# HGRN level scores by blocks of 64 keys, and retention decode states in the third weight set

## The chip, the cores and the metric

The kernel runs on one core of one Trainium2 chip. The metric is the device time of one execution in microseconds. The program before was run three times; the median is 1087.16 us. One more execution was taken by the hardware profiler. TensorE (PE) does the matmuls and its weight loads (PEld), VectorE (DVE) and ScalarE (ACT) the elementwise work, GpSimd (POOL) a little of it, and SyncE (SP) issues most DMAs.

## The reference

One inference step of a decoder layer, all in fp32: 2048 prompt tokens from an empty state, and 8 decode sequences of one token each, which start from stored states. The width is 1024. Four heads of 128 are RetNet retention (a fixed decay per head), four are HGRN2 (a forget gate per channel and token).

```python
h = rmsnorm(x, norm_g)
p = (h @ w_in).astype(jnp.float32)
rq, rk, rv, rg, hq, hf, hi, hgate = jnp.split(p, 8, axis=-1)
...
o_ret, s_ret_new = chunked_decay_recurrence(rq, rk, rv, log_gamma, s_ret)
o_ret = head_rmsnorm(o_ret, ret_g) * jax.nn.silu(rg)
...
logf = jnp.logaddexp(jnp.log(lbf), jnp.log1p(-lbf) + jax.nn.log_sigmoid(hf))
kin = (1.0 - lbf) * jax.nn.sigmoid(-hf)
hq_act = jax.nn.silu(hq)
o_hg, s_hg_new = chunked_decay_recurrence(
    hq_act.reshape(B, L, HG_HEADS, HG_DK), kin.reshape(B, L, HG_HEADS, HG_DK),
    hi.reshape(B, L, HG_HEADS, HG_DV), logf.reshape(B, L, HG_HEADS, HG_DK), s_hg)
o_hg = head_rmsnorm(o_hg, hg_g) * jax.nn.silu(hgate)
...
o_cat = jnp.concatenate([o_ret, o_hg], axis=-1).astype(x.dtype)
y = x + o_cat @ w_out
```

The recurrence of a head is S_t = diag(f_t) S_{t-1} + k_t v_t^T with o_t = S_t^T q_t. Results are the normed outputs of the prompt and of the decode tokens, and the new states of both.

## The kernel before

**Stages.** Matmuls of the large products are done in F32R with each operand split into a high and a low part, three products in place of one. The first 578 us project the prompt, pair by pair of 128-token chunks, with seven block products per pair (the list CHAIN, run by v_pair); eight pairs make one weight set. The first set (token pairs i = 0 to 7) gives values and decode projections, the second (8 to 15) the retention queries and gates, the third (16 to 23) the retention keys and the HGRN gates. In the third set the retention of the prompt runs along, one step between two block products (r_steps: r_flip transposes the keys into pkt, r_score and r_update make par and pur, r_out makes por and rS and the normed output obr, r_turn transposes it into potr). What is not done by its end is the list tail_f, which is emptied between the first projection steps of the scan (the list early).

Then comes the scan: eight units, one per HGRN head and half of the prompt. A unit projects its gate and query (pjf, pjq, line 879), while the unit before it is worked through by hgrn_rec. The output projection (py, po) ends the program.

**Levels.** Within a chunk of 128 tokens, hgrn_rec builds the matrix A of scores by levels: level b (1, 2, 4, ..., 64) holds the pairs whose query is in an odd block of b tokens and whose key is in the even block before it. After each level, update scales keys and queries by the products of the gates, in place. The five small levels, 1 to 16, are made by small: before, a chunk is cut into four blocks of 32 keys, and each is a matmul of 32 keys (the stationary operand, 128 rows by 32 columns) with the 16 queries of odd blocks among the same 32 tokens. Each fp32 matmul is two instructions with two weight loads. The four blocks of a chunk write to four ranges of 32 partitions in one bank of PSUM. What the level's mask allows is copied by put into the tile Ab (copy_predicated, line 1091). scores0 does the diagonal (pd, through the unit matrix id32) and level 1; scores(1) levels 2 and 4; scores(3) levels 8 and 16; scores3 levels 32 and 64 (p5 and p6) and the copies into A on ACT. They stand at fractions 0.08, 0.3, 0.52 and 0.74 of a unit, in bursts: all 64 or 128 small matmuls in a row. keep sets a copy of keys and queries aside for the first of two levels.

**Decode heads.** A head's decode state is a tile dS of 128 by 8 by 128. d_load fetches it and the values vb (dv), d_mul and d_add compute the new state on DVE, and d_mm stores it and multiplies it by the query (pd, line 563), copies the result (de) and writes it to d_dram. Before, all eight heads stand in the list side_at at places in units 4 to 7.

**What sets the order.** TensorE's order is the order of the program text. On the other engines a scheduler places instructions by their dependencies; behind(f) ties what f emits to what was last emitted on DVE, ACT and SP. Tiles of a pool with one tag share buffers in turn.

Of the kernel before, what the change touches and what calls it, by code (L numbers as in the profile page):

```python
# [18 lines left out]
P = 128  # L19
# [13 lines left out]
PACK = dict(gk=4, gkd=4, epsg=4, ng=8, hg_lb=8, id32=32, xs_t=64, lmask=16 * len(SMALL), causal=P)  # L33
# [8 lines left out]
def step_kernel(ctx, tc, a, out):  # L42
# [55 lines left out]
    gk, gkd, ng, epsg, causal, id32 = (packed(n) for n in ("gk", "gkd", "ng", "epsg", "causal", "id32"))  # L98
# [5 lines left out]
    lmask = const.tile([P, len(SMALL) * 16], U8, name="lmask")  # L104
# [570 lines left out]
    dve.tensor_copy(lmask, packed("lmask"))  # L675
# [106 lines left out]

    n_tok = len(TOK)
    SPLIT_AT = 3
    for i in range(2, n_tok):
# [232 lines left out]
    def hgrn_rec(half, h, u):  # L1018
# [53 lines left out]
        def small(dst, li, ss=None):  # L1072
            b = LEVELS[li]
            m = 32 // (2 * b)
            for c in range(CH):
                for i in range(4):
                    at = c * P + 32 * i
                    if ss is None:
                        kk = k[:, at : at + 32]
                        n0 = (c * 4 + i) * m  # L1080
# [4 lines left out]
                    pe.matmul(dst[32 * i : 32 * i + 32, c], kk, qq, start=True, stop=True)  # L1085

        def put(src, li):
            b = LEVELS[li]
            m = 32 // (2 * b)
            mk = lmask[:, li * 16 : (li + 1) * 16].rearrange("p (n b) -> p n b", b=b)  # L1090
            dve.copy_predicated(
                box["Ab"].rearrange("p c (n two b) -> p c n two b", two=2, b=b)[:, :, :, 1, :],
                mk.unsqueeze(1).to_broadcast([P, CH, m, b]),
                src.rearrange("p c (n b) -> p c n b", b=b),
            )

        def scores0():
            box["Ab"] = pools["up"].tile([P, CH, 32], F32, tag="Ab", name=f"Ab{name}")
            pa = ps_lv.tile([P, 2, CH, 32], F32, tag="lv", name=f"pa{name}")
            pd, p0 = pa[:, 0], pa[:, 1, :, :16]  # L1100
            for c in range(CH):
                for i in range(4):
                    cc = slice(c * P + 32 * i, c * P + 32 * i + 32)
                    pe.matmul(pd[32 * i : 32 * i + 32, c], k[:, cc], q[:, cc], start=True, stop=True)
            small(p0, 0)
            update(0)
            products()
            dve.tensor_tensor(
                box["Ab"], pd, id32.unsqueeze(1).to_broadcast([P, CH, 32]), op=ALU.mult
            )  # L1110
            put(p0, 0)
            keep(1)

        def scores(li):
            pl = ps_lv.tile([P, 2, CH, 16], F32, tag="lv", name=f"pl{name}{li}")
# [7 lines left out]
        def scores3():  # L1123
# [81 lines left out]
    dec = {}  # L1205

    def d_load(hd):
        ty, h = divmod(hd, NH)
        S = rawp.tile([P, NB, P], F32, tag="raw", name=f"dS{hd}")
        vb = rawp.tile([P, NB, P], F32, tag="raw", name=f"dv{hd}")  # L1210
        sp.dma_start(S, (a["state_ret"], a["state_hgrn"])[ty][0, :, h].rearrange("b d v -> d b v"))
        sp.dma_start(vb, vd_dram[ty, :, h * P : (h + 1) * P].partition_broadcast(P))
        dec["l", hd] = (S, vb)

    def d_mul(hd, n):
        ty, h = divmod(hd, NH)
        S, vb = dec["l", hd]
        if n == 0:
            kd = dk[:, hd].unsqueeze(2).to_broadcast([P, NB, P])
            dve.tensor_tensor(vb, vb, kd, op=ALU.mult)  # L1220
        elif ty == 1:
            fd = df[:, hd].unsqueeze(2).to_broadcast([P, NB, P])
            dve.tensor_tensor(S, S, fd, op=ALU.mult)

    def d_add(hd):
        ty, h = divmod(hd, NH)
        S, vb = dec["l", hd]
        if ty == 0:
            dve.scalar_tensor_tensor(S, S, GAMMA[h], vb, op0=ALU.mult, op1=ALU.add)
        else:  # L1230
            dve.tensor_tensor(S, S, vb, op=ALU.add)
        if hd == 0:
            dec["q"] = pools["up"].tile([P, 8, 32], F32, tag="dqp", name="dqp")
            dve.tensor_copy(dec["q"][:, :, 8:32], zero.unsqueeze(1).to_broadcast([P, 8, 24]))
            dve.tensor_copy(dec["q"][:, :, 0:8], dq)

    def d_mm(hd):
        S, vb = dec["l", hd]
        ty, h = divmod(hd, NH)
        sp.dma_start(out[("new_ret_sample", "new_hgrn_sample")[ty]][0, :, h].rearrange("b d v -> d b v"), S)  # L1240
        e = pools["tp"].tile([P, 512], F32, tag="tmp", name=f"de{hd}")
        pt = ps_o.tile([P, 256], F32, tag="o", name=f"pd{hd}")
        four(pt, dec["q"][:, hd], S.rearrange("p b d -> p (b d)"), True, True)
        act.activation(e[:, :256], pt, AF.Copy)
        for i in range(2):
            act.dma_start(d_dram[hd, i::2], e[i : i + 103 : 34, i * P : i * P + P])

# [54 lines left out]
    for hd, at in enumerate((4.22, 5.01, 5.24, 6.01, 6.16, 6.31, 7.01, 7.22)):  # L1302
# [107 lines left out]
    for i in range(len(order)):  # L1410
# [4 lines left out]
        if i == 0:  # L1415
# [306 lines left out]
def _layout(x_prompt, x_sample, state_ret, state_hgrn, norm_g, w_in, ret_norm_g, hg_norm_g,  # L1722
# [41 lines left out]
    arrays["id32"] = (i[:, None] % 32 == i[None, :32]).astype(f32)  # L1764
    masks = []
    s32 = i % 32
    for b in SMALL:
        t = np.array([x for x in range(32) if (x // b) % 2 == 1])
        masks.append((s32[:, None] // b + 1) == (t[None, :] // b))
# [24 lines left out]
```

## Time and profile before

| | us |
| --- | --- |
| three runs | 1086.08, 1087.16, 1093.3 |
| median | 1087.16 |
| profiled execution | 1087.88 |
| its span | 1086.1 |
| TensorE busy (page, part 1) | 1043.2 |
| DVE busy | 760.8 |
| ACT busy | 553.3 |

The profile is of one execution. Its span is the time from the first to the last instruction; 1.8 us of the execution lie outside it. "Busy" of TensorE counts time in which at least one matmul is in flight by the profiler's model. In the rows of groups, "128*32" is the shape of the weights, what follows it the operand; "x1024" counts instructions; after the bar stand the group's busy time, the mean nanoseconds of one instruction, the idle time just before them and what ended it. Buffer numbers are left out of names, so pl of unit h00 is plh.

### The profile page before, as it was taken

How to read it: one execution, taken by the hardware profiler on the slowest of the kernel's cores; microseconds unless marked ns; L12 is line 12 of the kernel's file. 1: busy time of each engine (PE TensorE's matmuls, PEld its weight loads, DVE VectorE, ACT ScalarE, POOL GpSimd, SP SyncE). 2: the span in 40 equal slices, each digit the busy share in tenths (PEclk: the TensorE clock that was granted, in tenths of full speed). 3: DMA queues.
4: the chain of work that ended last, by engine and by line, in shares of the span. 5: the costliest groups of instructions: out<-in, count | busy, mean ns of one | idle time of the engine just before them, and what ended most of it. 6: DMA issues, size and time to landing. Idle time of an engine off the chain costs nothing.

```text
span 1086.1 us, 22296 instructions
## 1 busy us (share of the span) xinstructions
PE 1043.2 (96%) x8743; PEld 860.5 (79%) x8743; DVE 760.8 (70%) x1400; ACT 553.3 (51%) x1204; POOL 127.9 (12%) x224
## 2 busy tenths in 40 slices
PE   9999999999999999999999989899999998999997
PEld 7778778787778788888887968787887877888775
DVE  6876765987667876666656676768657786568776
ACT  7853444643344755455555655565545573523242
POOL 1310001000001011111111100011012011221112
PEclk9999999999999999999999999999999998999999
DMA  8689989668769865555567686767577483496652
GB/s 296 209 296 318 339 286 324 229 221 302 257 225 285 290 228 175 162 172 174 168 204 273 211 287 221 282 192 228 182 211 214 141 269 110 130 357 200 213 172 97
DMA packets 147130, 248.34 MB, mean 229 GB/s; under 512 B 10608, under 2 KB 78464, under 8 KB 146768
## 3 DMA queue, kind: packets, MB, share of 16 engines
q1 hardware_dynamic: 139424, 221.34, 61.5%
q0 software_dynamic: 7328, 25.27, 6.6%
q8 instruction: 69, 1.13, 0.4%
q14 instruction: 37, 0.30, 0.1%
q10 hardware_dynamic: 272, 0.30, 0.1%
HBM read 162.32 MB, written 84.54 MB: 227 GB/s over the span
## 4 chain that ended last, share of the span: by engine, by line
PE 65%; DMA 13%; DVE 8%; ACT 7%; issue 4%; POOL 2%; SPq 1%; DVEq 0%; POOLq 0%; ACTq 0%
PE po L332 11%; PE pjfh L879 5%; PE pjqh L879 5%; DMA xn<-in_x_prompt 4%; PE py L1502 4%; DMA qt_dram<-qt 2%; PE par L702 1%; PE plh L1085 1%; PE pur L709 1%; PE por L715 1%; PE puh L960 1%; DMA wr<-in_w_in 1%; PE poh L976 1%; PE por L717 1%; DMA wg1B<-in_w 1%
## 5 line engine op out<-in xcount | busy, mean ns | idle before, releaser
L879 PE MATMUL pjqh<-xh,w_h 128*128 128x512 f32 (+2 forms) x160 | 60.5, 378 | 2.9 <-DVE qh L930 1.9
L879 PE MATMUL pjfh<-xh,w_h 128*128 128x512 f32 (+2 forms) x160 | 59.9, 374 | 0.0
L879 PE MATMUL pjfh<-xh,w_l 128*128 128x512 f32 (+2 forms) x160 | 57.0, 356 | 0.7 <-DVE w_l L116 0.7
L879 PE MATMUL pjfh<-xl,w_h 128*128 128x512 f32 (+2 forms) x160 | 57.2, 357 | 0.4 <-DVE xl L116 0.3
L1065 ACT ACTIVATE kepth<-kh 128x1024 f32<-128x1024 f32 x24 | 25.4, 1060 | 62.0 <-DVE kh L1055 58.2
L879 PE MATMUL pjqh<-xl,w_h 128*128 128x512 f32 (+2 forms) x160 | 56.7, 354 | 0.0
L879 PE MATMUL pjqh<-xh,w_l 128*128 128x512 f32 (+2 forms) x160 | 56.6, 354 | 0.0
L1055 DVE TENSOR_TENSOR kh<-kh,fph 128x512 f32<-128x512 f32 x48 | 33.4, 696 | 21.3 <-PE plh L1085 11.3
L116 DVE TENSOR_TENSOR ab_l<-xr,ab_h 128x512 fp32r<-128x512 f32 (+1 forms) x40 | 37.5, 953 | 6.9 <-ACT ab_h L115 6.9
L731 DVE SCALAR_TENSOR_TENSOR obr<-por,omr,rg 128x128 f32<-128x128 f32 x64 | 18.0, 344 | 34.1 <-POOL omr L729 34.1
L115 ACT ACTIVATE ab_h<-xr 128x512 fp32r<-128x512 f32 (+1 forms) x40 | 32.3, 840 | 17.1 <-DVE xr L286 17.0
L987 DVE SCALAR_TENSOR_TENSOR obh<-poh,orsh,v 128x128 f32<-128x128 f32 x64 | 18.0, 344 | 30.9 <-POOL orsh L112 30.9
L879 PEld LDWEIGHTS pjqh<-xh,w_h 128*128 128x128 f32 x160 | 30.6, 191 | 8.5 <-DVE qh L930 2.1
L879 PEld LDWEIGHTS pjfh<-xh,w_l 128*128 128x128 f32 x160 | 30.8, 192 | 5.9 <-DVE w_l L116 1.6
L879 PEld LDWEIGHTS pjfh<-xh,w_h 128*128 128x128 f32 x160 | 30.6, 191 | 5.5 <-issue 1.2
L879 PEld LDWEIGHTS pjfh<-xl,w_h 128*128 128x128 f32 x160 | 30.8, 193 | 4.3 <-DVE xl L116 1.0
L879 PEld LDWEIGHTS pjqh<-xh,w_l 128*128 128x128 f32 x160 | 30.7, 192 | 4.3
L286 DVE SCALAR_TENSOR_TENSOR xr<-xr,g_in,rb 128x256 f32<-128x256 f32 x64 | 26.7, 479 | 10.4 <-DMA xr<-in_x_t 5.0
L879 PEld LDWEIGHTS pjqh<-xl,w_h 128*128 128x128 f32 x160 | 30.8, 192 | 3.0
L1058 DVE TENSOR_TENSOR qth<-qth,fph 128x512 f32<-128x512 f32 x48 | 32.8, 684 | 0.0
L742 ACT ACTIVATE obr<-potr,pk 128x128 f32<-128x128 f32 x64 | 19.0, 368 | 21.7 <-PE potr L740 21.7
L1592 DVE SCALAR_TENSOR_TENSOR xro<-xro,yms,fg 128x1024 f32<-128x1024 f32 (+1 forms) x13 | 15.5, 1202 | 18.5 <-POOL yms L112 18.5
(1836 smaller groups left out, 3426.4 us busy)
## 6 DMA issues: line engine op xcount, KB each, us to landing
xr<-a_dram SPq DMA_DIRECT2D x24, 512.0 KB
S<-s_dram SPq DMA_DIRECT2D x24, 512.0 KB
xn<-in_x_prompt SPq DMA_DIRECT2D x32, 256.0 KB
xr<-in_x_t SPq DMA_DIRECT2D x16, 512.0 KB
a_dram<-xr SPq DMA_DIRECT2D x16, 512.0 KB
s_dram<-S SPq DMA_DIRECT2D x16, 512.0 KB
wgr<-in_w SPq DMA_DIRECT2D x16, 512.0 KB
xr<-a_dram SPq DMA_DIRECT2D x32, 256.0 KB
```

The costliest lines, as they stand in the source:

```text
L115: act.activation(h, src, AF.Copy)
L116: dve.tensor_tensor(l, src, h.bitcast(F32), op=ALU.subtract)
L286: dve.scalar_tensor_tensor(r[:, k], r[:, k], g_in[:, kk : kk + 1], spread_to[i], op0=ALU.mult, op1=ALU.mult)
L332: pe.matmul(ps, xx, ww, start=(first and n == 0), stop=(last and n == 2), skip_group_check=more)
L731: dve.scalar_tensor_tensor(o[:, cc], po[:, h], ms[:, h : h + 1], rb_of[c, "g"][:, cc], op0=ALU.mult, op1=ALU.mult)
L742: act.activation(o[:, cc], pt[:, h], AF.Copy, scale=ng[:, h : h + 1])
L879: pe.matmul(ps, ww[:, kk], x[:, k, b0 : b0 + n], start=(k == 0 and i == 0), stop=(k == KT - 1 and i == 2),)
L987: dve.scalar_tensor_tensor(ob[g][:, j], po[:, j], rs[:, j : j + 1], gcol(4 * g + j), op0=ALU.mult, op1=ALU.mult)
L1055: dve.tensor_tensor(kv[:, :, 0, :], kv[:, :, 0, :], two[:, :, 1:2].to_broadcast([P, nb, b]), op=ALU.mult)
L1058: dve.tensor_tensor(qv[:, :, 1, :], qv[:, :, 1, :], two[:, :, 0:1].to_broadcast([P, nb, b]), op=ALU.mult)
L1065: act.activation(ss[:, 512:], k[:, :HALF], AF.Copy)
L1502: pe.matmul(ps, o[:, kk], w[:, k % 4, i * 512 : (i + 1) * 512], start=(k == 0 and n == 0), stop=(k == KT - 1 and n == 2),)
```

## The change

**Blocks of 64 keys.** small cuts a chunk into two blocks of 64 keys, each multiplied by the 32 queries of odd blocks among the same 64 tokens. There are 640 such matmuls in place of 1280, in two column groups in place of four. Ab is 64 wide; put writes 256 elements per partition in place of 128; the diagonal, which stays in blocks of 32, is multiplied into Ab in two halves by id64; two copies bring Ab into A, and they stand before the copies of p5 and p6.

On TensorE, at the first burst of the first scan unit, the row pah (line 1104) is the diagonal and the next row level 1. Before:

```order
L879 MATMUL pjfh_512_5761<-xl_5561,w_h 128x256
L879 MATMUL pjfh_512_5761<-xh_5560,w_l 128x256
L1104 MATMUL pah_5775<-qh_5590,kh_5589 32x32 x32
L1085 MATMUL pah_5775<-qth_5591,kh_5589 32x16 x32
L879 MATMUL pjfh_512_5761<-xh_5560,w_h 128x256
L879 MATMUL pjfh_512_5761<-xl_5561,w_h 128x256
```

And with the change, where the lines are 63 further on:

```order
L942 MATMUL pjfh_512_5830<-xl_5630,w_h 128x256
L942 MATMUL pjfh_512_5830<-xh_5629,w_l 128x256
L1167 MATMUL pah_5844<-qh_5659,kh_5658 32x32 x32
L1148 MATMUL pah_5844<-qth_5660,kh_5658 64x32 x16
L942 MATMUL pjfh_512_5830<-xh_5629,w_h 128x256
L942 MATMUL pjfh_512_5830<-xl_5630,w_h 128x256
```

The burst stands at the same place; its second half is 16 matmuls with an output of 64 by 32 in place of 32 with one of 32 by 16. The bursts of scores(1) and scores(3) change alike.

**Retention decode heads.** The functions d_load to d_mm move up in the text, ahead of the loop over token pairs, and the four retention heads run with token pairs 18 to 22 of the third set: a load after block product 3, the multiplication after 4, the addition after 6, and the matmul after product 1 of the next pair, in a bank of the pool ps_tr. The HGRN heads stand at 4.4, 5.1, 5.9 and 6.6 of the scan. d_dram is written from SP's queue in place of ACT's. The load of a token pair's operands comes after product 5 in the third set, as in the second, in place of 2.

On TensorE, where pair 19 passes from its second to its third product, potr and pkt are transposes of the retention, pv19 products of the pair, and pd the decode matmul of head 0. Before:

```order
L740 MATMUL potr_4041<-ident,obr_3986 128x128 x4
L332 MATMUL pv19b<-wv_h,ab_h 128x512
L332 MATMUL pv19b<-wv_l,ab_h 128x512
L332 MATMUL pv19b<-wv_h,ab_l 128x512
L332 MATMUL pv19b<-wv_h,ab_h 128x512
L332 MATMUL pv19b<-wv_l,ab_h 128x512
L332 MATMUL pv19b<-wv_h,ab_l 128x512
L694 MATMUL pkt_4065<-ident,rk_4008 128x128 x4
L332 MATMUL pv19a<-T2h,s190h 128x512
```

And with the change:

```order
L742 MATMUL potr_4052<-ident,obr_3996 128x128 x4
L332 MATMUL pv19b<-wv_h,ab_h 128x512
L332 MATMUL pv19b<-wv_l,ab_h 128x512
L332 MATMUL pv19b<-wv_h,ab_l 128x512
L332 MATMUL pv19b<-wv_h,ab_h 128x512
L332 MATMUL pv19b<-wv_l,ab_h 128x512
L332 MATMUL pv19b<-wv_h,ab_l 128x512
L696 MATMUL pkt_4076<-ident,rk_4018 128x128 x4
L563 MATMUL pd_4088<-dS_3897,dqr 32x256 x4
L332 MATMUL pv19a<-T2h,s190h 128x512
```

pd stands between pkt and the next product, as it does in the three pairs that follow.

On DVE, from the retention of pair 18 to the keys of pair 19 (rS and obr belong to the retention, rk and t to the keys), before:

```order
L721 SCALAR_TENSOR_TENSOR rS<-rS,pur_3941 128x128 x4
L731 SCALAR_TENSOR_TENSOR obr_3986<-por_3973,omr_3987,rg_3920 128x128 x4
L349 TENSOR_TENSOR t_4009<-pv18a,rot_3744 128x512
L352 TENSOR_TENSOR t_4010<-pv18a,rot_3744 128x4x64
L353 SCALAR_TENSOR_TENSOR t_4010<-pv18a,rot_3744 128x4x64
L354 TENSOR_TENSOR rk_4008<-t_4009,t_4010 128x512
L384 TENSOR_TENSOR rk_4057<-pv19b,s_19_4030 128x512
```

And with the change, where dv and dS are head 0's values and state:

```order
L723 SCALAR_TENSOR_TENSOR rS<-rS,pur_3951 128x128 x2
L800 TENSOR_TENSOR dv_3898<-dv_3898,dk 128x1024
L723 SCALAR_TENSOR_TENSOR rS<-rS,pur_3951 128x128 x2
L733 SCALAR_TENSOR_TENSOR obr_3996<-por_3983,omr_3997,rg_3929 128x128 x4
L349 TENSOR_TENSOR t_4019<-pv18a,rot_3746 128x512
L352 TENSOR_TENSOR t_4020<-pv18a,rot_3746 128x4x64
L353 SCALAR_TENSOR_TENSOR t_4020<-pv18a,rot_3746 128x4x64
L354 TENSOR_TENSOR rk_4018<-t_4019,t_4020 128x512
L809 SCALAR_TENSOR_TENSOR dS_3897<-dS_3897,dv_3898 128x1024
L384 TENSOR_TENSOR rk_4068<-pv19b,s_19_4041 128x512
```

The multiplication of dv parts the four rS and stands ahead of obr; the addition into dS stands between the two keys.

**Smaller edits.** The mask lmask comes from an input of its own through a tile in vq, no longer out of the packed constants pk. A spare tile, fill, grows from 104 to 120 floats. As built, the tiles of the pools xp, wp, rawp, vq, vp, tp and up start at multiples of 512 bytes; before, 64 bytes beyond one. Of the list early, the entries after which a step of tail_f runs are 0, 1, 4, 6, 8 and 11 in place of 0, 1, 3, 5, 7 and 11.

```diff
-    gk, gkd, ng, epsg, causal, id32 = (packed(n) for n in ("gk", "gkd", "ng", "epsg", "causal", "id32"))
+    gk, gkd, ng, epsg, causal, id64 = (packed(n) for n in ("gk", "gkd", "ng", "epsg", "causal", "id64"))
...
-    const.tile([P, 104], F32, name="fill")
+    const.tile([P, 120], F32, name="fill")
...
-    dve.tensor_copy(lmask, packed("lmask"))
+    lm = vq.tile([P, GW], F32, tag="rv", name="lm")[:, : len(SMALL) * 32]
+    sp.dma_start(lm, a["lmask"])
+    dve.tensor_copy(lmask, lm)
...
+    def d_mm(hd):
+        S, vb = dec["l", hd]
+        ty, h = divmod(hd, NH)
+        sp.dma_start(out[("new_ret_sample", "new_hgrn_sample")[ty]][0, :, h].rearrange("b d v -> d b v"), S)
+        if ty:
+            e = pools["tp"].tile([P, 512], F32, tag="tmp", name=f"de{hd}")
+            pt = ps_o.tile([P, 256], F32, tag="o", name=f"pd{hd}")
+        else:
+            e = vq.tile([P, GW], F32, tag="xn", name=f"de{hd}", bufs=2)
+            pt = ps_tr.tile([P, 256], F32, tag="tr", name=f"pd{hd}")
+        four(pt, dec["q", ty][:, h], S.rearrange("p b d -> p (b d)"), True, True)
+        act.activation(e[:, :256], pt, AF.Copy)
+        for i in range(2):
+            sp.dma_start(d_dram[hd, i::2], e[i : i + 103 : 34, i * P : i * P + P])
...
-            at = 5 if i % N_V > 2 and i < 2 * N_V else 2
+            at = 5 if i % N_V > 2 else 2
...
+        if i == 2 * N_V + 2:
+            after[0] += [lambda: d_pad(0)]
+        hd = i - 2 * N_V - 2
+        if 0 <= hd < NH:
+            after[3] += [lambda hd=hd: d_load(hd)]
+            after[4] += [lambda hd=hd: behind(lambda: d_mul(hd, 0))]
+            after[6] += [lambda hd=hd: behind(lambda: d_add(hd))]
+        if 0 < hd <= NH:
+            after[1] += [lambda hd=hd: d_mm(hd - 1)]
...
         def small(dst, li, ss=None):
             b = LEVELS[li]
-            m = 32 // (2 * b)
+            m = 64 // (2 * b)
             for c in range(CH):
-                for i in range(4):
-                    at = c * P + 32 * i
+                for i in range(2):
+                    at = c * P + 64 * i
...
-                        kk = ss[:, 512 + at : 512 + at + 32]
-                        qq = ss[:, at // 2 : at // 2 + 16]
-                    pe.matmul(dst[32 * i : 32 * i + 32, c], kk, qq, start=True, stop=True)
+                        kk = ss[:, 512 + at : 512 + at + 64]
+                        qq = ss[:, at // 2 : at // 2 + 32]
+                    pe.matmul(dst[64 * i : 64 * i + 64, c], kk, qq, start=True, stop=True)
...
-            mk = lmask[:, li * 16 : (li + 1) * 16].rearrange("p (n b) -> p n b", b=b)
+            mk = lmask[:, li * 32 : (li + 1) * 32].rearrange("p (n b) -> p n b", b=b)
...
-            box["Ab"] = pools["up"].tile([P, CH, 32], F32, tag="Ab", name=f"Ab{name}")
+            box["Ab"] = pools["up"].tile([P, CH, 64], F32, tag="Ab", name=f"Ab{name}")
...
-            dve.tensor_tensor(
-                box["Ab"], pd, id32.unsqueeze(1).to_broadcast([P, CH, 32]), op=ALU.mult
-            )
+            for j in range(2):
+                jj = slice(32 * j, 32 * j + 32)
+                dve.tensor_tensor(
+                    box["Ab"][:, :, jj], pd, id64[:, jj].unsqueeze(1).to_broadcast([P, CH, 32]), op=ALU.mult
+                )
...
+            for i in range(2):
+                pp = slice(64 * i, 64 * i + 64)
+                act.activation(A[pp, :, pp], box["Ab"][pp], AF.Copy)
             for i in (0, 64):
                 act.activation(A[i : i + 32, :, i + 32 : i + 64], p5[i : i + 32], AF.Copy)
             act.activation(A[0:64, :, 64:128], p6, AF.Copy)
-            for i in range(4):
-                pp = slice(32 * i, 32 * i + 32)
-                act.activation(A[pp, :, pp], box["Ab"][pp], AF.Copy)
...
-    for hd, at in enumerate((4.22, 5.01, 5.24, 6.01, 6.16, 6.31, 7.01, 7.22)):
+    side_at.append((4.1, lambda: d_pad(1)))
+    for hd, at in zip(range(NH, 2 * NH), (4.4, 5.1, 5.9, 6.6)):
...
-                if n in (0, 1, 3, 5, 7, 11):
+                if n in (0, 1, 4, 6, 8, 11):
```

More of the change, by code (lines that the diff above doesn't have):

```diff
@@ L32 @@
 SMALL = [1, 2, 4, 8, 16]
-PACK = dict(gk=4, gkd=4, epsg=4, ng=8, hg_lb=8, id32=32, xs_t=64, lmask=16 * len(SMALL), causal=P)
+PACK = dict(gk=4, gkd=4, epsg=4, ng=8, hg_lb=8, id64=64, xs_t=64, causal=P)
 PACK_AT = {n: sum(list(PACK.values())[:i]) for i, n in enumerate(PACK)}
@@ L103, in step_kernel @@
     lb1 = const.tile([P, NH], F32, name="lb1")
-    lmask = const.tile([P, len(SMALL) * 16], U8, name="lmask")
+    lmask = const.tile([P, len(SMALL) * 32], U8, name="lmask")
     rs_all = const.tile([P, T // P], F32, name="rs_all")
     rsd = const.tile([NB, 2], F32, name="rsd")
-    const.tile([P, 104], F32, name="fill")
+    const.tile([P, 120], F32, name="fill")
     dq, dk, df = (const.tile([P, 8, NB], F32, name=f"d{n}") for n in "qkf")
@@ L1114, in scores @@
         def scores(li):
-            pl = ps_lv.tile([P, 2, CH, 16], F32, tag="lv", name=f"pl{name}{li}")
+            pl = ps_lv.tile([P, 2, CH, 32], F32, tag="lv", name=f"pl{name}{li}")
             small(pl[:, 0], li, box["kept"])
@@ L1203, in t_store @@
             sp.dma_start(t_dram[x, n][:, :, k], y.bitcast(F32).rearrange("p (a b) -> p a b", a=2))
[L1205 to L1246, printed above, removed]
     def d_norm():
@@ L1763, in _layout @@
     arrays["causal"] = (i[:, None] <= i[None, :]).astype(f32)
-    arrays["id32"] = (i[:, None] % 32 == i[None, :32]).astype(f32)
+    arrays["id64"] = (i[:, None] % 64 == i[None, :64]).astype(f32)
     masks = []
-    s32 = i % 32
+    s64 = i % 64
     for b in SMALL:
-        t = np.array([x for x in range(32) if (x // b) % 2 == 1])
-        masks.append((s32[:, None] // b + 1) == (t[None, :] // b))
+        t = np.array([x for x in range(64) if (x // b) % 2 == 1])
+        masks.append((s64[:, None] // b + 1) == (t[None, :] // b))
     arrays["lmask"] = np.concatenate(masks, 1).astype(f32)
```

40 lines of the change are left out of this document (36 added, 4 removed).

## The prediction

> **What bounds the kernel now.** I read the page first, then the table of windows, the waits of TensorE, and single stretches of its timeline.
>
> ```profile
> PE 1043.2 (96%) x8743; PEld 860.5 (79%) x8743; DVE 760.8 (70%) x1400; ACT 553.3 (51%) x1204; POOL 127.9 (12%) x224
> ...
> q8 instruction: 69, 1.13, 0.4%
> ...
> 372.00:578.00 206.00, 204.93 (x1185) 176.08 (x1184) 137.32 (x304) 112.40 (x320) 28.83 (x42) 1.00 0.58 186
> ...
> 684.00:728.00 44.00, 37.98 (x641) 33.80 (x639) 28.44 (x61) 24.39 (x52) 3.59 (x6) 0.96 0.70 233
> ...
> sum 382.00, PE 356.78 PEld 302.47 DVE 261.28 ACT 209.20 POOL 48.66; mean PE 44.60 PEld 37.81 DVE 32.66 ACT 26.15 POOL 6.08
> ```
>
> The window rows give the stretch and its length, then busy time of PE, PEld, DVE, ACT and POOL, the granted clock, the DMA share and GB/s. TensorE is the bound nearly everywhere (1043.2 of 1086.1 us). The third weight set, 372 to 578, leaves it 1.1 us idle: whatever TensorE is given there is paid in full, and whatever makes it wait as well. The scan, 578 to 960 (the sum row: eight stretches, 382 us), leaves it 25.2 us idle, very unevenly: 6.0 of them in the 44 us from 684. The scan is where the change can win, so its waits come next:
>
> ```profile
> PE plh L1085 <- issue: 10.7, 4, 4.1
> PE pd L563 <- DVE dS L1231: 2.4, 1, 2.4
> PE pkt L694 <- DVE rk L354: 2.2, 1, 2.2
> PE plh L1130 <- issue: 1.9, 1, 1.9
> ...
> PE pd L563 <- DVE obh L987: 1.0, 2, 0.6
> ```
>
> (Us in total, times, longest.) Half of the idle time, 10.7 + 1.9 = 12.6 us, was spent waiting for "issue", which is nothing the profile shows. The timeline has one such stop inside a burst of level matmuls:
>
> ```profile
> 659.50 0.62 PE L1085 MATMUL plh<-qth,kh 128*32 128x16 f32 x52
> 661.95 0.27 PE L1085 MATMUL plh<-qth,kh 128*32 128x16 f32 x10 [1.84 <-issue]
> ```
>
> The first 52 of one tile's matmuls run, then 1.84 us pass, then the last 10. Their operands were complete before the first, so no data was missing. I take it that the instructions were: by the queue row one of the 69 packets holds 1.13 MB / 69 = 16.4 KB, and 17,486 instructions (8743 matmuls, 8743 loads) in 1.13 MB are 64.6 bytes each, so 254 to a packet. My own count along the trace puts all of these stops at the same place modulo 256 instructions, and each ends some 2.5 us after an instruction packet starts. What follows such a stop is dearer than it looks:
>
> ```profile
> 639.10:642.50 3.40, 3.17 (x22) 3.08 (x23) 3.34 (x5) 2.83 (x4) 0.00 (x0) 0.51 0.28 103
> 663.00:666.40 3.40, 3.40 (x18) 3.40 (x18) 1.81 (x5) 2.01 (x4) 0.00 (x0) 0.50 0.90 337
> 704.00:707.40 3.40, 3.21 (x14) 2.62 (x15) 2.81 (x6) 1.58 (x2) 0.00 (x0) 0.50 0.98 315
> 874.70:878.10 3.40, 3.40 (x10) 2.63 (x9) 3.40 (x7) 1.79 (x4) 0.00 (x0) 0.50 0.96 253
> 902.00:908.80 6.80, 4.27 (x33) 3.67 (x34) 3.38 (x8) 1.58 (x2) 0.57 (x1) 0.50 0.05 15
> ```
>
> These five stretches were granted half the clock (third column from the right). The first three and the last come with an issue stop, the fourth with the 2.4 us wait of pd.
>
> **The change part by part.** *Level matmuls.* The new ones have 64 weight columns in two column groups; none exists in the trace. The neighbours:
>
> ```profile
> 673.00 0.70 PE L1085 MATMUL plh<-kepth 128*32 128x16 f32 x62
> ...
> 673.56 0.70 PE L1085 MATMUL plh<-qth,kh 128*32 128x16 f32 x62
> ...
> 679.45 0.70 PE L1130 MATMUL plh<-kepth 128*32 128x32 f32 x32
> 680.08 1.15 PE L1135 MATMUL plh<-qth,kh 128*64 128x64 f32 x16
> ...
> 680.18 0.98 PE L1135 MATMUL plh<-qth,kh 128*64 128x64 f32 x14
> ...
> L1104 PE MATMUL pah<-qh,kh 128*32 128x32 f32 x512 | 6.1, 199 | 0.0
> L1085 PE MATMUL pah<-qth,kh 128*32 128x16 f32 x512 | 6.1, 184 | 0.0
> ...
> L1135 PE MATMUL plh<-qth,kh 128*64 128x64 f32 x128 | 10.0, 236 | 1.2 <-DVE qth L1058 1.2
> ...
> L563 PE MATMUL pd<-dS,dqp 128*32 128x256 f32 x64 | 5.1, 391 | 3.4 <-DVE dS L1231 2.4 <-DVE obh L987 1.0
> ...
> 873.41 0.64 PE L563 MATMUL pd<-dS,dqp 128*32 128x256 f32 x8 [2.36 <-DVE dS L1231]
> ```
>
> Now: a level of one unit is 64 instructions (8 chunks, 4 blocks, 2 each) in 0.56 us (673.00 to 673.56), 8.75 ns each; the four column groups overlap, so a group takes one every 35 ns. L1130, two groups of 32 columns: with some 0.20 us for one alone (L1104's mean), (0.70 − 0.20)/31 = 16.1 ns, 32 ns a group. L1135, one group of 64 columns: (0.98 − 0.236)/13 = 57 ns. Is it the 64 columns or the 64 queries that make it 57? Queries cost little: 512 matmuls with 32 of them (L1104) and with 16 are both busy 6.1 us; and pd, with 256 moving columns over four groups, is spaced (0.64 − 0.391)/7 = 36 ns, 142 a group, 0.56 ns a column, so that 64 queries need only 36 of the 57 ns. The weight columns set the pace. So a new instruction takes 57 ns in its group and 28.6 with two groups side by side; a level is 32 × 28.6 = 0.915 us against 0.56, and 5 levels × 8 units × 0.355 = **+14.2 us**. Halving the instructions makes this matmul work longer. Bounds: by L1130's 16.1 ns, 0.52 a level and −1.7 in all; without overlap of the two groups 57 × 32 = 1.82, +50. I take the 28.6, as L1135 alone has the column count.
>
> The Trainium skill says this more strictly (TensorE: Matmul & The Clock Gate, LDWEIGHTS): a load takes columns / 1.2 ns, whatever the rows. From that page I estimate 53 ns per 64 columns and 27 per 32, which makes the term +17 instead of +14; the trace's 57 and 35 are nearby, with a fixed part the rule lacks.
>
> *Tile shape.* In scores0 the diagonal matmuls stay at 32 columns and level 0 is 64: one more switch in a burst. From L1130 to L1135 (679.45 to 680.08) 0.63 us pass for 32 × 16.1 = 0.52 us of matmuls: 0.1 each, 8 units, **+0.8**.
>
> *Issue stops.* A pair of levels now runs through 256 instructions, loads counted, in 1.12 us, faster than the 2.5 us of a packet; afterwards 128 in 1.83 us, a packet's worth in 3.6. Supply is then quicker than demand. I expect 12 of the 12.6 us to go and a rest to stay where bursts lie close (scores3's are unchanged): **−12**. At half clock the work takes twice its time, so a stretch costs half its busy time: (3.17 + 3.40 + 3.21 + 4.27)/2 = 7.0, of which I keep a quarter: **−5.3**. If the stops are not fetching, both stay (rival 2).
>
> *Decode heads and DVE.* Retention heads 0 to 3 leave the scan; the four HGRN heads stand alone instead of up to three within 0.3 of a unit.
>
> ```profile
> L1091 DVE COPY_PREDICATED Abh<-lmask,plh 128x128 f32<-128x128 uint8 x32 | 10.5, 329 | 0.3
> ...
> L1108 DVE TENSOR_TENSOR Abh<-pah,pk 128x256 f32<-128x256 f32 x8 | 3.3, 418 | 0.0
> ...
> L1220 DVE TENSOR_TENSOR dv<-dv,dk 128x1024 f32<-128x1024 f32 x8 | 9.7, 1218 | 0.0
> ...
> L1229 DVE SCALAR_TENSOR_TENSOR dS<-dS,dv 128x1024 f32<-128x1024 f32 x4 | 4.9, 1218 | 0.0
> ...
> 443.66 0.39 PE L332 MATMUL pv19a<-T2l,s190h 128*128 128x512 f32 x1
> 443.89 0.40 PE L332 MATMUL pv19a<-T2h,s190l 128*128 128x512 f32 x1
> ```
>
> put writes 256 elements instead of 128. L1220 and L1108 differ by 768 elements and 800 ns, so 128 more cost 0.13 us, 40 × 0.13 = 5.3; the second id64 product adds 8 × 0.418 = 3.3; four heads leave 4.9 + 4.9 = 9.8 behind. DVE's sum in the scan falls by 1 us, but put now stands longer ahead of the update of qth, for which L1135 already waited 1.2 us. Between 0 and 8 × 0.65 = 5.2 (five puts of 0.13 more, none hidden); in 382 us L1135 was late once, so **+1**. The pd waits were 2.4 + 1.0, and the dip of 874.7 costs 3.40/2 = 1.7; with heads further apart I let 3 of these 5.1 go: **−3** (0 if the same add is still late). The third set's last pkt comes one block of six matmuls later (the early steps run at 4, 6, 8 instead of 3, 5, 7); products of 512 columns start 0.23 us apart (the last two rows), 6 × 0.23 = 1.4 against its 2.2 us wait: **−1.4**.
>
> *Third set.* pd (0.64 us a head, by its row at 873.41) only moves, net 0. Its mul and add have to fit:
>
> ```profile
> 438.46 1.12 DVE L731 SCALAR_TENSOR_TENSOR obr<-por,omr,rg 128x128 f32<-128x128 f32 x4 [2.33 <-POOL omr L729]
> ...
> 440.88 0.69 DVE L354 TENSOR_TENSOR rk<-t,t 128x512 f32<-128x512 f32 x1
> 443.25 0.69 DVE L384 TENSOR_TENSOR rk<-pv19b,s 128x512 f32<-128x512 f32 x1 [1.69 <-PE pkt L694]
> ...
> 445.38 0.69 DVE L354 TENSOR_TENSOR rk<-t,t 128x512 f32<-128x512 f32 x1
> ...
> 441.79 1.15 ACT L742 ACTIVATE obr<-potr,pk 128x128 f32<-128x128 f32 x4 [1.15 <-PE potr L740]
> 442.98 0.60 PE L694 MATMUL pkt<-ident,rk 128*128 128x128 f32 x4
> ```
>
> The mul (1.2 us) stands between two pairs of rS, ahead of obr, which waits 2.33 us for POOL anyhow; the add (1.2) falls into the 1.69 us before 443.25. pd needs the bank that ACT frees at 442.94, and its place comes after pkt, at 443.34: just in time. Queued behind it on TensorE are the products. One head costs 0 to 1 us: **+1.2** for four, bounds 0 and 4. SP gains the waits for dS and de, with loads of xr and S for the token pair after next behind them, most of a token pair (206/8 = 26 us) ahead of use: 0. ACT's copies of Ab fall from four of a quarter to two of a half and come first: 0, since A's reader, oo, comes in the next unit.
>
> *Mask load and addresses.* 80 KB under the first products, one small copy: 0. As built, the main pools stand at 64 modulo 512 bytes before, at 0 after. The rk of 445.38 lies in such a pool, that of 440.88 in one that was at 0 already; both take 0.69. I take 0. DMA is the other end:
>
> ```profile
> 76.00:208.00 132.00, 127.41 (x603) 100.43 (x603) 88.53 (x139) 62.25 (x102) 8.87 (x19) 0.99 0.89 314
> ```
>
> here, at DMA 0.89, quicker transfers could win at most the 4.6 us that TensorE idles.
>
> **Sum**, against the profiled execution's 1087.88: 14.2 + 0.8 − 12 − 5.3 − 3 − 1.4 + 1.2 + 1 = −4.5, so 1083.4. The median of the runs is 0.7 lower (1087.16), so 1082.7: **1083**. Two large terms nearly cancel.
>
> **The rivals.** (1) *Columns don't set the pace.* If L1130's 16.1 ns holds, the +14.2 becomes −1.7 and the time is 1067. For it: 16 and 32 queries cost the same, so a fixed price per instruction is not excluded below 64 columns. Against it: the 57 ns, which queries don't explain.
> (2) *Slower: the stops are not fetching.* Something else at level bursts holds TensorE, the stops and their half clocks stay, and the longer bursts are paid in full: 1082.7 + 12 + 5.3 = 1100. It decides once over 10.6 of the 17.3 us stay (below that the result is within 1%). Against: the stop between two matmuls of one tile, and the common place modulo 256. The Trainium skill speaks for this rival (Runtime: NRT & Kernel Launch, Instruction fetch mechanics): crossing a 16 KiB block is called mostly hidden. By that rule the sum would be this rival's; the trace's 1.84 us within a burst disagrees.
> (3) *Slower: two 64-column groups don't overlap*: +50 instead of +14.2, 1119. Against: groups of 32 overlap in twos and fours.
> (4) *The third set waits.* The four vb loads start late, and each head holds TensorE as pd did once, 2.4 us: 4 × 2.4 on top, 1092.
>
> **How the numbers follow.** My forecast has 0.60, with a range of its own from 1075 to 1092 (third set 4 instead of 1.2, pd waits unchanged, up to four more us of stops above; addresses −4.6 and all stops gone below). Rival 1 has 0.15, rival 2 0.15, rival 3 0.05, rival 4 0.05. From 1067 to 1101 leaves out only rival 3 and the tails. About 1% (11 us) is what a measurement of this kernel can tell from no change: faster means below 1076, slower above 1098. Faster: rival 1 and 0.06 of the forecast's lower tail, 0.21. Slower: rivals 2 and 3 and 0.02 of the upper tails, 0.22. The rest, 0.57, is within 1%.
>
> **What would show it.** L1148's matmuls (the new line of the levels) about 0.9 us for 32 instructions of a level; 0.52 would be rival 1, 1.8 rival 3. "issue" ahead of level matmuls under 2 us in all, and no half-clock stretch in the middle of a unit; 10 or more would be rival 2. TensorE idle at most 3 us between 372 and 578. No pd wait over 1 us. What would make it wrong most easily is the price of 64 columns: 5 ns per instruction are 6 us.

## The result and the profile after

Seven runs of the changed kernel have a median of 1078.79 us (1076.5 to 1083.33) against 1086.08 us for seven runs of the kernel before: the ratio is 0.9929, with a 95% interval from 0.9901 to 0.9957. That is 7.3 us less, where 4.5 less were forecast. The time lies within the range and under 1% from before. The profiled execution took 1076.5 us, the shortest of the seven, with a span of 1074.6, and the profiled execution of before took 1087.88, longer than the median. The two profiles are therefore 11.5 us apart where the medians are 7.3 apart; stages are compared with care, and the sizes of effects come from the runs.

The page's busy row and its row of the instruction queue, then TensorE's waits in the scan (579 to 954):

```profile
PE 1048.1 (98%) x7463; PEld 868.6 (81%) x7463; DVE 771.5 (72%) x1410; ACT 550.1 (51%) x1188; POOL 124.4 (12%) x224
...
q8 instruction: 59, 0.97, 0.4%
```

```profile
PE plh L1200 <- DVE qth L1121: 2.2, 3, 1.5
PE plh L1195 <- ACT kepth L1129: 1.3, 1, 1.3
PE pjfh L942 <- DVE xl L116: 1.2, 4, 0.7
...
PE pd L563 <- DVE obh L1050: 0.3, 1, 0.3
...
PE pkt L696 <- DVE rk L354: 0.2, 1, 0.2
```

TensorE issues 1280 matmul instructions fewer and is busy 4.9 us longer. Of "issue" there is no row left: before, 12.6 us. The pd waits (3.4) are down to 0.3. New at the top are waits of the last burst of a unit for DVE and ACT, 3.5 us in all.

The scan's window before (the third set's, 206.00 long, is in the prediction), then the windows of the third set and of the scan with the change, which start and end at the same matmuls:

```profile
578.00:960.00 382.00, 356.78 (x5242) 302.47 (x5241) 261.28 (x534) 209.20 (x464) 48.66 (x75) 0.97 0.67 215
...
369.30:579.40 210.10, 207.66 (x1217) 176.59 (x1216) 145.80 (x312) 114.04 (x324) 29.73 (x42) 1.00 0.66 212
579.40:949.35 369.95, 362.29 (x3930) 310.25 (x3929) 263.68 (x534) 204.49 (x444) 48.03 (x75) 1.00 0.61 204
```

(5242 matmuls less the 1280 and less the 32 of the four decode heads are 3930.) The third set became 4.1 us longer and the scan 12.0 shorter; the scan's granted clock is 1.00 in the mean, where it was 0.97, and TensorE idles 7.7 us of it in place of 25.2. The mean granted clock of the whole execution went from 0.988 to 0.998.

The new level matmuls, in the timeline and as groups:

```profile
658.75 1.12 PE L1148 MATMUL plh<-kepth 128*64 128x32 f32 x32
659.70 1.10 PE L1148 MATMUL plh<-qth,kh 128*64 128x32 f32 x32
660.73 0.39 PE L942 MATMUL pjfh<-xh,w_h 128*128 128x256 f32 x1
...
L1148 PE MATMUL plh<-kepth 128*64 128x32 f32 x512 | 18.0, 224 | 0.0
L1148 PE MATMUL plh<-qth,kh 128*64 128x32 f32 x512 | 17.7, 223 | 0.1
...
L1148 PE MATMUL pah<-qth,kh 128*64 128x32 f32 x256 | 9.0, 224 | 0.0
```

A level takes 0.95 us from its first matmul to the next level's first, and (1.12 − 0.224)/31 = 28.9 ns separate two instructions; 28.6 was taken. The old groups, from the table of groups of before (the third, pah with 6.1 us, is in the prediction):

```profile
L1085 PE MATMUL plh<-qth,kh 128*32 128x16 f32 x1024 | 12.9, 186 | 11.0 <-issue 10.7 <-DVE qth L1058 0.4
L1085 PE MATMUL plh<-kepth 128*32 128x16 f32 x1024 | 11.9, 185 | 0.4 <-DVE sth L968 0.4
```

In all, 18.0 + 17.7 + 9.0 = 44.7 us against 12.9 + 11.9 + 6.1 = 30.9: 13.8 us more, where 14.2 were forecast.

### The profile page after: what moved, and what is told of

The parts are those of the page before. It is cut to its first block, busy times and chain, and to the rows that moved or that the text cites. A ratio compares the mean times of both kernels' runs of the same rounds, so it can differ in the third digit from the quotient of the medians.

```text
span 1074.6 us, 19750 instructions
## 1 busy us (share of the span) xinstructions
PE 1048.1 (98%) x7463; PEld 868.6 (81%) x7463; DVE 771.5 (72%) x1410; ACT 550.1 (51%) x1188; POOL 124.4 (12%) x224
```

## The experiments

Each ratio is to the kernel before, run on the same chip beside it. The theory at the start was the prediction's: the levels cost 14 us more on TensorE and get back 17 because instructions arrive in time; decode heads and addresses matter little. Its rivals were that the stops of TensorE have another cause, or that the gain comes from something else in the change.

**Small levels back at 32 keys (e1).** Everything else as changed.

```diff
-            m = 64 // (2 * b)
+            m = 32 // (2 * b)
...
-                for i in range(2):
-                    at = c * P + 64 * i
+                for i in range(4):
+                    at = c * P + 32 * i
```

> The changed kernel with its small levels back at blocks of 32 keys; decode heads, addresses, mask load and early steps as changed. Theory (64 columns cost 28.6 ns an instruction, and the issue stops come from instruction supply): the level bursts get 15 us shorter, 8 to 16 us of issue stops and some 5 us of half clock come back; time 1077 to 1084, about level with the changed kernel's 1079. Rival (the stops went with the decode heads' move or the addresses): under 2 us of issue stops and 1064.

Ratio 0.9941 (0.9917 to 0.9964), median 1080.22 us. The stops come back:

```profile
PE plh L1148 <- issue: 13.7, 5, 4.3
```

The row is from the profiled execution, which took 1087.62 us, the longest of the nine; the stops of a usual one may be fewer. The time fits the theory and not the rival's 1064. But it sits uneasily beside the changed kernel's 0.9929: without the 64-key levels six tenths of a per cent were already won, and by something that the theory gave nothing.

**64-key levels alone (e2).** The kernel before with the new small, put, scores0 and scores, the mask by its own load, and the spare tile sized so that the pools stay at 64 beyond multiples of 512.

```diff
-    const.tile([P, 104], F32, name="fill")
+    const.tile([P, 132], F32, name="fill")
```

> The kernel before with its small levels at blocks of 64 keys and nothing else changed (addresses still 64 beyond multiples of 512 bytes). Theory: issue stops before level matmuls fall under 2 us and the bursts get 15 us longer; pd still waits over 1 us; time 1080 to 1087 against 1086 before. Rival (stops independent of instruction density): 10 us or more of issue stops, 1101.

Ratio 0.9954 (0.9932 to 0.9976), median 1081.87 us. No issue row is left in the scan, and the mean granted clock is 0.996 in place of 0.988. The rival that forecast 1101 falls. The levels alone win some 5 us.

**Addresses alone (e3).** The kernel before with one number changed:

```diff
-    const.tile([P, 104], F32, name="fill")
+    const.tile([P, 88], F32, name="fill")
```

> The kernel before with the spare tile 16 floats smaller, which brings the main pools to multiples of 512 bytes, and nothing else. Theory: the address costs nothing, 1083 to 1088, first weight set within 1 us of before. Rival (the address carries the gain): 1079 or less, with the first 186 us 2 us or more shorter.

Ratio 0.9952 (0.9932 to 0.9972), median 1081.42 us: the theory was wrong, and 64 bytes are worth as much as the levels. The rival's second half is wrong too: the first weight set, from its third token pair's first product to the next set's, is only 1.5 us shorter (128.4 against 129.9), and in the kernel before it holds a stretch of 3.4 us at half clock (from 151.0) that e3 has not. The gain is found on TensorE itself. In the output projection twelve products of 512 columns lie between each of these rows and the next; first the kernel before, then e3:

```profile
996.94 0.39 PE L332 MATMUL po<-woh,op4A11h 128*128 128x512 f32 x1
...
999.66 0.39 PE L332 MATMUL po<-woh,op4A11h 128*128 128x512 f32 x1
...
1002.46 0.39 PE L332 MATMUL po<-oT2h,op4S2h 128*128 128x512 f32 x1
```

```profile
993.37 0.39 PE L332 MATMUL po<-woh,op4A11h 128*128 128x512 f32 x1
...
996.09 0.39 PE L332 MATMUL po<-oT2h,op4S2h 128*128 128x512 f32 x1
```

Before, the first twelve products of these tiles take 2.72 us, 227 ns each, and the second twelve 2.80, 233 ns each; with the pools at multiples of 512 the second twelve are 227 ns apart too. So the address slows some products of a tile and not others. Over all products of this size that follow one another into the same tile (some 2800 gaps of 200 to 260 ns in each trace), the mean fell from 229.9 to 228.8 ns: some 3.2 us of the 5.2. The products of the scan's projections nearly keep their mean spacing (pjf with xl and w_h 233.5 and 232.9 ns): the rows of x are 528 floats apart, 2112 bytes, 64 beyond a multiple of 256, so that in both kernels most of them start off such a multiple. The length of one product shows none of this: these rows say 0.39 in both kernels.

**64 instructions earlier (e4).** The kernel before with sixteen tiny matmuls more in the warm-up, which shift the instruction stream and nothing else.

```diff
+    for n in range(16):
+        g = 32 * (n % 4)
+        pe.matmul(wu[g : g + 32, :16], ones[:, :32], ones[:, :16], start=True, stop=True)
```

> The kernel before with 16 tiny matmuls more (64 instructions on TensorE, loads counted) in the warm-up at the start, which moves everything after by 64 places in the instruction stream. Theory (instruction supply): stops of the same sort, 8 to 18 us in sum, but at other bursts or other places within bursts, 64 instructions earlier in the work. Rival (a stop belongs to a place in the program): the same stops before the same matmuls with the same lengths within 0.3 us.

One run, 1090.82 us. Two bursts of e4, where TensorE stops:

```profile
668.22 0.35 PE L1088 MATMUL plh<-qth,kh 128*32 128x16 f32 x20
670.54 0.57 PE L1088 MATMUL plh<-qth,kh 128*32 128x16 f32 x42 [1.97 <-issue]
...
708.14 0.38 PE L1088 MATMUL plh<-qth,kh 128*32 128x16 f32 x24
709.48 0.52 PE L1088 MATMUL plh<-qth,kh 128*32 128x16 f32 x38 [0.95 <-issue]
```

and the second one in the kernel before (the first, x52 and x10, is in the prediction):

```profile
699.40 0.65 PE L1085 MATMUL plh<-qth,kh 128*32 128x16 f32 x56
704.19 0.30 PE L1085 MATMUL plh<-qth,kh 128*32 128x16 f32 x6 [4.14 <-issue]
```

The stop moved from after 52 to after 20 matmuls, and from after 56 to after 24: 32 matmuls with their 32 loads, exactly the 64 instructions put in. Counted from the start of the execution, 4024 matmuls lie ahead of the first stop in both kernels and 4660 ahead of the second. A stop keeps its place in the instruction stream and leaves its place in the work; its length changes (4.14 to 0.95). All stops of e4 at level matmuls come to 10.6 us. A wait for data would have stayed with its matmul; a supply of instructions in packets would move like this. Each of the four stops ends 2.3 to 2.5 us after a packet of the instruction queue starts (659.5 and 701.7 before, 668.0 and 707.2 in e4).

**64-key levels and addresses together (e5).** e2 with 116 floats in the spare tile; decode heads and early steps as before.

> The kernel before with 64-key levels and the main pools at multiples of 512 bytes; decode heads and early steps as before. Theory (levels and addresses gain separately, 5.1 and 5.6 us in the two runs that had one alone; the decode move costs the third set more than it gives back): 1075 to 1078, at or below the changed kernel's 1079. Rival (the decode move is worth something in the scan): 1081 or more.

Ratio 0.9906 (0.9884 to 0.9928), median 1075.71 us: the two add up, and the kernel without the decode move is at least as fast as the changed one.

**Split bursts of 32 keys (e6).** e3 with each burst cut in two, a block of six or more projection matmuls between.

```diff
-        levels = [(0.08, scores0), (0.3, lambda: scores(1)), (0.4, load), (0.52, lambda: scores(3)),
+        levels = [(0.08, scores0a), (0.145, scores0b), (0.3, lambda: scoresa(1)), (0.365, lambda: scoresb(1)), (0.4, load),
+                  (0.455, lambda: scoresa(3)), (0.52, lambda: scoresb(3)),
```

> The kernel before with aligned pools, 32-key levels, and each burst of two levels cut in two with at least one block of six projection matmuls between the halves (same instructions, same number of them). Theory (a burst outruns the instruction supply; a gap lets it catch up): issue stops under 4 us in all, bursts stay at 8.75 ns an instruction, 1081.4 of the aligned run less 10 to 17: 1064 to 1071. Rival (the 32-column matmuls themselves stop, whatever their spacing): stops of 10 us or more, 1080 to 1083.

Ratio 0.9932 (0.9907 to 0.9957), median 1077.99 us. The stops behave as forecast; the time is 7 us above the forecast's upper end:

```profile
PE plh L1143 <- DVE qth L1058: 4.6, 3, 3.9
PE plh L1085 <- issue: 3.2, 3, 1.8
PE plh L1085 <- ACT kepth L1066: 3.0, 2, 1.7
PE pd L563 <- DVE dS L1240: 2.2, 1, 2.2
```

Issue falls to 3.2 us, from 12.6 in e3: a gap lets the supply catch up. But by the first and third row TensorE now waits 7.6 us for the updates on DVE and the copies on ACT, and these take the place of the stops.

**The changed kernel, 64 instructions earlier (e7).** The same sixteen matmuls in the changed kernel.

> The changed kernel with 64 more instructions on TensorE at the start. Theory (64-key bursts are slower than the supply): no issue stop over 0.8 us before or within level matmuls, wherever the packets fall. Rival (the changed kernel's packets merely fell well): one stop of 1.5 us or more within a burst.

One run, 1078.25 us; no issue row in the scan. The packets fall elsewhere here, so the changed kernel's freedom from stops doesn't hang on where they fell.

**The changed kernel with split bursts of 32 keys (e8).**

> The changed kernel with 32-key levels in split bursts. Theory: as the split kernel without the decode move, plus what that move costs, 1066 to 1073, issue stops under 4 us. Rival: 1080, as with 32-key levels unsplit.

Ratio 0.9896 (0.9875 to 0.9916), median 1073.83 us, with 0.4 us of issue stops. The time is just above the 1066 to 1073 that were forecast, and one part of the forecast failed: the decode move was to add to the time of e6, and e8, which is e6 with that move (and the early steps and the mask's load), is 0.36% below it (uncertain by 0.3). Like e6 it waits for DVE and ACT, here 9.5 us in three rows:

```profile
PE plh L1207 <- DVE qth L1121: 4.8, 3, 4.1
PE plh L1202 <- ACT kepth L1129: 2.8, 1, 2.8
PE plh L1148 <- ACT kepth L1129: 1.9, 1, 1.9
```

**The changed kernel with its pools back at 64 bytes beyond (e9).**

```diff
-    const.tile([P, 120], F32, name="fill")
+    const.tile([P, 136], F32, name="fill")
```

> The changed kernel with its main pools put back to 64 bytes beyond multiples of 512 (the spare tile 16 floats larger). Theory (a product whose operand tiles start 64 bytes off takes 2 to 3 ns longer): 3 to 6 us slower than the changed kernel, 1081 to 1085; the output projection's products 230 ns apart, as in the kernel before, where the aligned run has 227. Rival (the aligned run's gain was something else in the kernel before, a transfer or a stop): 1079 and 227 ns.

Ratio 0.9995 (0.9973 to 1.0017), median 1087.39 us: without the addresses the change gains nothing. The loss is larger than the forecast's upper end, 1085. (The profiled execution, the longest of the twelve, also has two stretches at half clock in the third set, after waits of 1.9 and 2.1 us for rq.) The output projection's twelve products take 2.80 us again:

```profile
1000.26 0.39 PE L332 MATMUL po<-woh,op4A11h 128*128 128x512 f32 x1
...
1003.06 0.39 PE L332 MATMUL po<-oT2h,op4S2h 128*128 128x512 f32 x1
```

**256 bytes beyond (e10).** 56 floats in the spare tile.

> The changed kernel with its main pools 256 bytes beyond multiples of 512 (the spare tile 64 floats smaller). If any multiple of 256 does, 1079 and 227 ns between the output projection's products; if only multiples of 512 do, 1081 to 1085 and about 230 ns.

Ratio 0.9913 (0.9886 to 0.994), as with multiples of 512, and 226.7 ns between the same products. Multiples of 256 do.

**Other places for the split bursts (e11).** 0.06, 0.125, 0.285 and 0.35 for the first four halves, 0.76 for the last burst.

> The changed kernel with 32-key levels in split bursts, the first halves a little earlier in the unit and the last burst (levels 32 and 64) later, at 0.76 in place of 0.74. Theory (what is left of the gain is spent on waits for DVE and ACT ahead of the bursts, about 9 us): these fall by half, 1069 to 1073. Rival (the bursts' places don't matter): 1074, as with the first split.

Ratio 0.9884 (0.985 to 0.9918), median 1074.79: not to be told from e8, and with the rival. The waits moved rather than fell: 8.7 us, of which 2.8 now ahead of the diagonal.

**Retention heads later in the third set (e12).** e8 with this:

```diff
-            after[3] += [lambda hd=hd: d_load(hd)]
-            after[4] += [lambda hd=hd: behind(lambda: d_mul(hd, 0))]
-            after[6] += [lambda hd=hd: behind(lambda: d_add(hd))]
+            after[6] += [lambda hd=hd: d_load(hd)]
         if 0 < hd <= NH:
-            after[1] += [lambda hd=hd: d_mm(hd - 1)]
+            after[0] += [lambda hd=hd: behind(lambda: d_mul(hd - 1, 0))]
+            after[2] += [lambda hd=hd: behind(lambda: d_add(hd - 1))]
+            after[3] += [lambda hd=hd: d_mm(hd - 1)]
```

It was made because in e9 TensorE waited 5.1 us in the third set for loads of rq, and SP's queue there reads:

```profile
444.69 0.39 SPq L825 DMA_DIRECT2D out_new_ret_sample<-dS  x1
445.12 0.58 SPq L791 DMA_DIRECT2D dS<-in_state_ret  x1
449.93 0.36 SPq L792 DMA_DIRECT2D dv<-vd_dram  x1
...
454.75 0.32 SPq L691 DMA_DIRECT2D rq<-qt_dram  x1
```

dv's load waits over 4 us for the store of the head before, whose buffer it takes, and rq's load stands behind it.

> The split kernel with the decode move (32-key levels, aligned pools), with the four retention heads' work placed so that a head's two loads are issued three block products or more after the store of the head before: load after product 6, multiplication after product 0 of the next pair, addition after 2, store and matmul after 3. Theory (in the moved place the load of dv waits on SP's queue for the store of the head before, and the load of the retention's queries, rq, stands behind it): no wait of SP for that store, par waits under 1 us in all for rq, the third set 2 to 4 us shorter (about 226 us), 1070 to 1072. Rival (the four heads' 4 MB of transfers slow rq wherever they stand): third set still 229 to 231, time 1074.

Ratio 0.9879 (0.9848 to 0.9911), median 1073.33. SP's waits for that store fell from 9.4 us in e8 to 1.0, but par still waits 2.0 us for rq (2.5 in e8), and the third set takes 228.3 us from its first product to the scan's, against 228.7. The wait on SP was there; it was not what cost the time. The expectation failed, nearer to its rival.

## Why the prediction was right, and which steps were not

The total was right within its range, and the mechanism of the levels held, but three terms were off by some 4 to 6 us each. The runs form a table for it:

| | pools 64 beyond | pools at 512 |
| --- | --- | --- |
| 32 keys, decode before | 1 | 0.9952 (e3) |
| 64 keys, decode before | 0.9954 (e2) | 0.9906 (e5) |
| 32 keys, decode moved | not run | 0.9941 (e1) |
| 64 keys, decode moved | 0.9995 (e9) | 0.9929 (changed) |
| 32 keys split, decode before | not run | 0.9932 (e6) |
| 32 keys split, decode moved | not run | 0.9896 (e8) |

Each difference of two entries is uncertain by about 0.3%. Going from 1 by e3 and e5 to the changed kernel, the addresses give −5.2 us, the levels −5.0 and the decode move +2.5, where 0, −1.3 and −3.2 were forecast. The errors partly cancel: that the total missed by 3 us only is luck.

**Mask load and addresses: "I take 0".** This is the step that failed. Its evidence was a DVE product that takes 0.69 us at either address; nothing was looked up for TensorE, which sets the time. The addresses are worth 0.48, 0.48 and 0.66% in the three pairs, 5 to 7 us, where the whole change gains 0.71%. The lower bound kept, −4.6, came from transfers in the first set and held the size almost by accident.

**Level matmuls: +14.2.** Right: 13.8 by the groups. Rivals 1 (16.1 ns) and 3 (57 ns) fall at 28.9 ns.

**Issue stops: −12 and −5.3.** The mechanism held (e2, e4, e6, e7), the first size too (12.6 to 0). The second was a little too small: all five stretches at half clock that the prediction lists are gone, and by its own count those of the issue stops were worth 7.0 us; a quarter was held back for nothing. The stretch after pd, 1.7 us, went as well. Rival 2 falls.

Together the levels were put at 14.2 + 0.8 − 12 − 5.3 + 1 = −1.3 us. In the pairs they are worth 0.46, 0.46 and 0.12%: 5, 5 and 1 us; the three agree within their uncertainty.

**Decode heads: −3, −1.4 and +1.2.** The single waits went as forecast (pd 3.4 to 0.3, pkt in the scan 2.2 to 0.2). Yet the move as a whole, with the early steps and in two pairs the mask's load, is worth −0.11% from e3 to e1 and −0.36% from e6 to e8, where the levels have 32 keys, but +0.23% from e5 to the changed kernel and +0.41% from e2 to e9, where they have 64. The forecast gain of 3.2 us is found in one pair of four, and not in the one that leads to the changed kernel. Why the sign differs stays open. What the move costs stands in the third set. TensorE there, in the changed kernel:

```profile
440.02 0.60 PE L696 MATMUL pkt<-ident,rk 128*128 128x128 f32 x4
440.80 0.64 PE L563 MATMUL pd<-dS,dqr 128*32 128x256 f32 x8 [0.19 <-ACT rk L699]
441.37 0.50 PE L332 MATMUL pv19a<-T2h,s190h 128*128 128x512 f32 x1
```

The same place before, with pkt's row (442.98) in the prediction:

```profile
443.34 0.48 PE L332 MATMUL pv19a<-T2h,s190h 128*128 128x512 f32 x1
```

From pkt to the next product it was 443.34 − 442.98 = 0.36 us; with pd between it is 441.37 − 440.02 = 1.35 for head 0, and 1.10 for each of the other three. The four heads cost 3.2 us there in place of the 4 × 0.64 = 2.6 that were moved; "just in time" was 0.19 us too late, for the first head alone. In the profiles with the pools at multiples of 512, the third set takes 222.8 to 225.5 us from its first product to the scan's with the decode heads in the scan (e3, e5, e6), and 228.7 to 231.0 with the move (the changed kernel, e1, e8, e11): in the mean 5.7 us more, of which 3.2 are pd's. TensorE's idle time there, 0.9 to 2.9 us in the profiles without the move and 2.7 to 5.7 in those with it, makes up most of the rest. What it is due to stays open: traffic is heavier there (0.66 against 0.58 of the DMA engines' time), but no run changed that alone, and e12 shows that SP's wait for the store is not it. The scan gives part of it back: from e5 to the changed kernel, which differ by this move and the early steps alone, the third set is 3.8 us longer and the scan 2.1 shorter. The waits for DVE and ACT ahead of the last bursts came to 3.5 us where 1.2 stood: the term of +1 for them was too small by a little. Rival 4 (the four heads' loads hold up the third set) falls by its price: TensorE idles 2.4 us in the third set's window in place of 1.1, where 9.6 were put on top.

## What to carry to other kernels

Before a change is costed, look at where its tiles come to lie: 16 floats in a spare tile were worth as much here as the redesign that they came with, and it is the spacing of TensorE's products that shows it, not the length of one. A burst of tiny matmuls can outrun its own instructions; fewer and longer ones, or a few large ones between, both cure it, and the choice is between TensorE's time (13.8 us here) and the wait of the chain behind a split (7.6 to 9.5 us). A total that comes out right says little about its terms: here the addresses' −5.2 had been put at 0, the levels' −5.0 at −1.3, and the decode move's +2.5 at −3.2.

The fastest versions are the split ones with aligned pools and the decode move, 0.9896, 0.9884 and 0.9879, which agree within their intervals; the interval of each overlaps the changed kernel's. A split version whose last burst doesn't wait for DVE was not found.

## What the runs showed of the hardware that was not expected

- With their pools 64 bytes beyond a multiple of 512, part of TensorE's F32R products are further apart: 233 ns in place of 227 in the second twelve of the 24 products with woh, wol and op4A11 (the first twelve are 227 apart in both kernels), 228.5 in place of 227.3 in the mean with oT2, and nearly no change in the mean with x, whose rows are 2112 bytes apart. 256 bytes beyond cost nothing (e10); no other distance was run. Whether it is the weights or the moving operand was not tried, nor rows of x at a better pitch.
- The place of an issue stop is fixed in the instruction stream (52 to 20 and 56 to 24 matmuls with 64 instructions put in front); its length is not (1.84 and 1.97 us, 4.14 and 0.95).
- Half the clock can follow a pause of TensorE for data as well, and the length of the pause alone doesn't decide. In e8 a wait of 4.1 us for DVE (until 642.27) and one of 1.9 us for ACT (until 630.08) were followed by it, a wait of 2.8 us for ACT (until 757.40) was not:

```profile
630.10:633.50 3.40, 3.40 (x70) 2.75 (x70) 0.80 (x2) 0.00 (x0) 0.00 (x0) 0.50 0.99 275
642.30:645.70 3.40, 3.40 (x23) 3.28 (x24) 2.57 (x4) 1.61 (x2) 0.00 (x0) 0.50 1.06 414
...
757.40:760.80 3.40, 3.28 (x60) 2.58 (x61) 1.96 (x3) 3.31 (x9) 0.27 (x1) 1.00 0.87 329
```

The traces show what goes with it. In each execution all stretches at half clock begin on one grid of 3.41 us. In the fourteen traces, between 30 and 1070 us, every grid window at full clock in which TensorE was idle for over 0.57 of the time was followed by a window at half clock (28 of 28), and none in which it was idle for under 0.47 (4162); in between, 13 were followed by one and 15 were not. e8's wait of 4.1 us left TensorE idle for 0.64 of the window from 636.9; its wait of 2.8 us fell on two windows, 0.54 and 0.33 of them. This is a count over these traces; no run moved a pause on the grid. In the changed kernel no pause in the scan is over 1.6 us, and none is followed by half the clock.
